# New-token attention: keys turned in blocks of 32 by VectorE, scores on 32 by 32 squares, values on quarters of the columns

## The chip, the cores and the metric

The kernel runs on one core of a Trainium2 chip. The core has five engines with instruction queues of their own: TensorE (PE in the profile, its weight loads PEld), VectorE (DVE), ScalarE (ACT), GpSimd (POOL) and SyncE (SP, which here only issues DMAs). TensorE multiplies on an array of 128 rows (the contracted index) by 128 columns (the output's partitions); a product can be put on a part of it. The metric is the device time of one launch in microseconds, median of three runs.

## The reference

A decoder step of two layers, on 512 prompt tokens and on eight sequences of eight new tokens each. The change is in the second layer's attention for the new tokens. Every new token has 16 heads of 64 in four groups (KV heads), and attends to three things: compressed keys, chosen blocks of 64 past keys, and a window of 512 keys. The last two are what the changed code computes:

```python
s = jnp.einsum('bqgrd,bqgksd->bqgrks', qg, kv_sel[..., 0, :])      # chosen blocks of the past 2048
p = masked_softmax(s, m.reshape(B, Q, KV_HEADS, 1, k_sel * SEL_BLOCK))
o_slc = jnp.einsum('bqgrks,bqgksd->bqgrd', p, kv_sel[..., 1, :])
s = jnp.einsum('bqgrd,bmgd->bqgrm', qg, wkv[:, :, 0])              # window
p = masked_softmax(s, wm[None, :, None, None, :])
o_win = jnp.einsum('bqgrm,bmgd->bqgrd', p.astype(wkv.dtype), wkv[:, :, 1])
o = g[..., 0:1] * o_cmp + g[..., 1:2] * o_slc + g[..., 2:3] * o_win
```

The kernel does not gather the chosen blocks: it computes the scores of all 2048 past keys and adds a large negative number to those of blocks not chosen. All of it is in 32-bit floats.

## The kernel before

The program runs these stages one after the other: pooling mixer, first feed-forward net, projections, compression of the past keys and values (`rounds`), new-token attention (`attend`), prompt attention, output projection, second feed-forward net. A scheduler orders the instructions of each engine, roughly as the code is written; a tile's buffer is handed on when its last reader has ended.

`attend` makes 40 steps, five for each of eight sequences b. Step 0 of a sequence is the window (512 rows of keys and values from `state_win_kv`), steps 1 to 4 are each 512 rows of the paged cache. A step's rows are one tile `sr` of 128 partitions, four rows in each, 1024 KB. `load` fetches it: the window by a DMA on SP, which also writes the shifted window to the output (`out_win_kv_s`, 1008 KB); the cache rows by a gather that POOL issues (L815). There are twelve such buffers, five in the pool `raws` that is open from earlier on, and seven (`more`) in memory that the stage before partly still uses.

- `prepare` (L1187 to L1201) turns the keys: eight PE transposes of 128 by 128 (`pk`), copied from PSUM to `kf` by ScalarE (two heads) and VectorE (the other two). It is done one step ahead.
- `score` (L1210 to L1235) multiplies them by the queries `qbd`, which hold two heads of 64 each on the rows and zeros in the other half: two products of 64 output partitions and 512 columns, side by side on the halves of the columns (`pss`). VectorE adds the mask and takes the maximum (`sc`, L1228, L1231). After step 0 and step 4 follows a softmax, whose exponential is one ScalarE instruction of 512 or 2048 elements (L1246).
- `turn` (L1252 to L1262) turns the probabilities back, four PE transposes (`ppt`), and `evac` copies them to `ph`, in turns by ScalarE and VectorE.
- `values` (L1265 to L1280): eight products of 64 by 128, on halves of the columns, into `po`. A pair of heads is multiplied with the values of both, so that half of each result is not used. They come six steps after the keys (four for the window), and are the last readers of `sr`.
- `outputs`, `outputs2`: the gates, and one transpose (`pot`) into `oS`.

All PSUM tiles of this and the stage before come from one group of eight banks (`any`). The weights of the output projection (`rawb`) and the prompt's keys and values (`kvt`) are loaded at the end of `attend`, as its memory comes free.

Of the kernel before, what the change touches and what calls it, by code (L numbers as in the profile page):

```python
# [60 lines left out]
def shape_constants():  # L61
# [36 lines left out]
    key = 4 * p[None, :] + np.arange(4)[:, None]  # L98
    parts["wm"] = np.where(key.reshape(1, -1) <= tt[:, None], NEG, 0.0)
# [30 lines left out]
def body(tc, top, I, O):  # L130
# [692 lines left out]
    def compress_setup(ctx):  # L823
# [21 lines left out]
        def buffers():  # L845
            xt = Z["xt"] = Slots(ctx, "xt", "right", hs=1, hgh=2, hgl=2, cvf=2)
            for n in range(XB):
                for tag in ("xf", "xhi", "xlo"):
                    xt.reserve(f"{tag}{n}", 1)
# [205 lines left out]
    def sample_attention(ctx):  # L1055
# [5 lines left out]
        VT = sa.tile([128, 2, 2, 128], F32, name="VT")  # L1061
# [12 lines left out]
        with ExitStack() as c1:  # L1074
# [6 lines left out]
            for j in range(2):  # L1081
                c0 = KC + 512 * (j + 1) + 256
                sp.dma_start(VT[64 * j:64 * j + 64, :, j], pjd[:, c0:c0 + 256].rearrange("t (a c) -> t a c", a=2))
# [102 lines left out]
        def prepare(i):  # L1186
# [5 lines left out]
            kf = kp_.tile([128, 2, 512], F32, tag="kf", name=f"kf{b}{ch}")  # L1192
            for p in range(2):
                pk = tpt(f"pk{b}{ch}{p}")
                for j in range(4):
                    transpose(pk[:, j * 128:(j + 1) * 128], raw[:, j, p * 128:(p + 1) * 128])
                if p:
                    dve.tensor_copy(kf[:, p], pk)
                else:
                    act.activation(kf[:, p], pk, AF.Copy)  # L1200
            kv[b, ch] = (kf, raw)  # L1201

        def attend(between):
# [4 lines left out]
            st, pend, po = {}, {}, {}  # L1208

            def score(i):  # L1210
# [13 lines left out]
                pt = mmt(f"pss{b}{ch}")  # L1224
                scores(pt, b, kf)
                if ch:
                    bias = sx[:, 128 * (ch - 1):128 * ch].unsqueeze(1).broadcast_to([128, 4, 128])
                    dve.tensor_tensor_reduce(sc[:, ch].rearrange("p (j k) -> p j k", j=4), pt.rearrange("p (j k) -> p j k", j=4),  # L1228
                                             bias, 1.0, -3e38, OP.add, OP.max, mx[:, ch - 1:ch])
                else:  # L1230
                    dve.tensor_tensor_reduce(sc[:, 0], pt, C("wm"), 1.0, -3e38, OP.add, OP.max, mx[:, 5:6])  # L1231
# [20 lines left out]
            def turn(b, ch):  # L1252
# [4 lines left out]
                for j in range(n):  # L1257
                    src = sc[:, ch, j * 128:(j + 1) * 128] if ch < 5 else (pcg[:, b] if j == 0 else pt_t)
                    transpose(pp[:, j * 128:(j + 1) * 128], src)
                ph = ptp.tile([128, 4, 128], F32, tag="ph", name=f"ph{b}{ch}")  # L1260
                evac(ph[:, :n].rearrange("p j c -> p (j c)"), pp[:, :n * 128])
# [3 lines left out]
            def values(b, ch):  # L1265
# [5 lines left out]
                for j in range(4 if ch < 5 else 2):  # L1271
                    for p in range(2):
# [515 lines left out]
```

## Time and profile before

| | us |
|---|---|
| median of 3 runs | 1693.01 (1692.02 to 1696.52) |
| profiled execution | 1694.61 |
| its span, first to last instruction | 1692.8 |
| PE busy in the span | 1628.4 (96%) |
| DVE, ACT, POOL busy | 1006.9, 766.5, 405.4 |
| mean granted clock of PE | 0.987 of 2.4 GHz |

The profile is of one execution. Its views: the page (busy times, groups of instructions by line), stretches (busy time of each engine in a window), the timeline, waits (who waited for whom) and DMA issues. A PE record is one pass: a 32-bit product shows as two records, a transpose as one. Records overlap, so how long a block takes is read from the start of the next one, not from its own duration. Times are counted from the span's start.

### The profile page before, as it was taken

How to read it: one execution, taken by the hardware profiler on the slowest of the kernel's cores; microseconds unless marked ns; L12 is line 12 of the kernel's file. 1: busy time of each engine (PE TensorE's matmuls, PEld its weight loads, DVE VectorE, ACT ScalarE, POOL GpSimd, SP SyncE). 2: the span in 40 equal slices, each digit the busy share in tenths (PEclk: the TensorE clock that was granted, in tenths of full speed). 3: DMA queues.
4: the chain of work that ended last, by engine and by line, in shares of the span. 5: the costliest groups of instructions: out<-in, count | busy, mean ns of one | idle time of the engine just before them, and what ended most of it. 6: DMA issues, size and time to landing. Idle time of an engine off the chain costs nothing. (4 is left out here: it accounts for less than half of the span.)

```text
span 1692.8 us, 31210 instructions
## 1 busy us (share of the span) xinstructions
PE 1628.4 (96%) x12663; PEld 1503.9 (89%) x12663; DVE 1006.9 (59%) x2052; ACT 766.5 (45%) x1400; POOL 405.4 (24%) x602
## 2 busy tenths in 40 slices
PE   8999999999999998999999998899999999999995
PEld 8999999999999998999966664556999999999995
DVE  7666364544474356888755547776456546454547
ACT  5655343343353324656554436666155524344331
POOL 3222021111020013334312206664023202111104
PEclk9999999999999998999999998999999999999998
DMA  5233133223246827454559971003312222222211
GB/s 191 84 101 100 51 100 101 75 76 100 64 138 213 253 88 282 156 190 168 181 179 348 341 204 25 1 2 90 94 51 97 79 75 94 82 82 78 91 60 57
DMA packets 121888, 204.95 MB, mean 121 GB/s; under 512 B 17327, under 2 KB 97289, under 8 KB 111376
## 3 DMA queue, kind: packets, MB, share of 16 engines
q1 hardware_dynamic: 111840, 133.45, 24.9%
q0 software_dynamic: 9216, 67.11, 11.0%
q10 hardware_dynamic: 688, 2.40, 0.4%
q8 instruction: 99, 1.62, 0.4%
q14 instruction: 45, 0.37, 0.1%
HBM read 178.58 MB, written 24.84 MB: 120 GB/s over the span
## 5 line engine op out<-in xcount | busy, mean ns | idle before, releaser
L166 PE MATMUL u<-xl,wha 128*128 128x288 f32 x704 | 208.1, 296 | 0.3 <-POOL xl L352 0.2
L166 PE MATMUL u<-xl,whb 128*128 128x288 f32 x704 | 208.1, 296 | 0.2
L166 PE MATMUL u<-xh,whb 128*128 128x288 f32 x704 | 207.4, 295 | 0.0
L166 PE MATMUL u<-xh,wha 128*128 128x288 f32 x704 | 207.4, 295 | 0.0
L166 PE MATMUL u<-xh,wla 128*128 128x288 f32 x704 | 207.3, 295 | 0.0
L166 PE MATMUL u<-xh,wlb 128*128 128x288 f32 x704 | 207.3, 295 | 0.0
L418 POOL COPY fcol<-u 128x18 f32<-128x18 f32 x88 | 68.4, 786 | 468.0 <-ACT u L417 468.0
L423 DVE SCALAR_TENSOR_TENSOR c<-u,convp,c 128x592 f32<-128x592 f32 x88 | 72.3, 831 | 122.5 <-ACT c L422 122.4
L258 DVE TENSOR_TENSOR wla<-rawa,wha 128x2048 fp32r<-128x2048 f32 (+1 forms) x52 | 99.5, 1918 | 69.3 <-ACT wha L257 69.3
L258 DVE TENSOR_TENSOR wlb<-rawb,whb 128x2048 fp32r<-128x2048 f32 x37 | 84.8, 2293 | 87.4 <-ACT whb L257 84.2
L166 PEld LDWEIGHTS u<-xl,wha 128*128 128x128 f32 x704 | 132.0, 188 | 2.0 <-DVE xl L352 1.1
L166 PEld LDWEIGHTS u<-xl,whb 128*128 128x128 f32 x704 | 132.0, 188 | 1.9 <-DVE xl L352 1.1
L166 PEld LDWEIGHTS u<-xh,wha 128*128 128x128 f32 x704 | 132.0, 188 | 0.1
L166 PEld LDWEIGHTS u<-xh,whb 128*128 128x128 f32 x704 | 132.0, 188 | 0.1
L166 PEld LDWEIGHTS u<-xh,wla 128*128 128x128 f32 x704 | 132.0, 188 | 0.0
L166 PEld LDWEIGHTS u<-xh,wlb 128*128 128x128 f32 x704 | 132.0, 188 | 0.0
L257 ACT ACTIVATE wha<-rawa 128x2048 fp32r<-128x2048 f32 (+1 forms) x52 | 83.0, 1615 | 91.3 <-PE d L166 58.9
L257 ACT ACTIVATE whb<-rawb 128x2048 fp32r<-128x2048 f32 x37 | 70.8, 1914 | 115.0 <-PE d L166 39.1
L504 DVE SCALAR_TENSOR_TENSOR xz<-xz,d 128x288 f32<-128x288 f32 x160 | 70.3, 450 | 86.7 <-PE d L166 85.9
L911 PE MATMUL pr<-xhi,W1h 128*128 128x256 f32 x512 | 105.6, 288 | 9.4 <-ACT xhi L884 9.4
L884 ACT ACTIVATE xhi<-xf 128x1024 fp32r<-128x1024 f32 (+1 forms) x68 | 70.1, 1031 | 80.0 <-PE pr L911 43.4
L882 DVE STREAM_TRANSPOSE xf<-cr 128x512 f32<-128x512 f32 x128 | 84.8, 691 | 33.9 <-POOL xlo L886 26.8
(657 smaller groups left out, 4640.6 us busy)
## 6 DMA issues: line engine op xcount, KB each, us to landing
rawa<-in_ffn_w_up SPq DMA_DIRECT2D x22, 1024.0 KB
rawb<-in_ffn_w_up SPq DMA_DIRECT2D x22, 1024.0 KB
rawa<-in_ffn_w_down SPq DMA_DIRECT2D x11, 1024.0 KB
rawb<-in_ffn_w_down SPq DMA_DIRECT2D x11, 1024.0 KB
rawa<-in_nsa_w_in SPq DMA_DIRECT2D x9, 1024.0 KB
sr<-in_state_win_kv SPq DMA_DIRECT2D x8, 1024.0 KB
out_win_kv_s<-sr SPq DMA_DIRECT2D x8, 1008.0 KB
rawb<-in_nsa_w_o SPq DMA_DIRECT2D x16, 256.0 KB
```

What stands on the lines that cost most here:

```text
L166: pe.matmul(out, a, b, start=first and j == 0, stop=last and j == n - 1)
L257: act.activation(h[:, a:b], r[:, a:b], AF.Copy)
L258: dve.tensor_tensor(lo[:, a:b], r[:, a:b], f32(h[:, a:b]), OP.subtract)
L418: pool.tensor_copy(col[:, :, m].rearrange("p (j i) -> p j i", i=2), u[:, TP:TP + 90].rearrange("p (j i) -> p j i", i=10)[:, :, 0:2])
L423: dve.scalar_tensor_tensor(c, u[:, 1:1 + CW], cv[:, 44 + m:45 + m], c, OP.mult, OP.add)
L504: dve.scalar_tensor_tensor(z, z, ALPHA if first else 1.0, p_[:, :HALF], OP.mult, OP.add)
L882: dve.transpose(xf[:, :, :, :, 32 * q:32 * q + 32].rearrange("p t d g n -> p t g d n"), src)
L884: act.activation(xhi.rearrange(flat), xf.rearrange(flat), AF.Copy)
L911: pe.matmul(banks[b, kv][ri][:, :, gh * nn:(gh + 1) * nn], W1[wi][:, kv, ri * 8 + th * 4 + c], xx[:, c // 2, c % 2].rearrange("p g n -> p ...
```

## The change

The keys no longer go through PE. One VectorE instruction turns each 32 by 32 block of a step's keys where it stands, so that the 64 elements of a head come to lie as two halves f of 32 rows, in each of the four row groups q of the array, and a row group holds 128 of the step's 512 keys. The queries are brought into the same form once (`qq`): sixteen small DMAs put them into rows of four heads by eight tokens, three DMAs repeat them for the other row groups, and VectorE turns them. The scores are then 32 products of 32 rows, 32 columns (a KV head's four heads by eight tokens) and 128 keys: for both halves f, each row group q and each KV head g one, on the square (q, g) of the array. Each row group writes into a bank of its own, and a step takes a quarter of each of four banks, in turn (`ring`). Keys are now numbered by partition first, so the mask of the window, the mask's broadcast and the slices of `turn` change to match.

The values become 16 products of 64 columns, one per KV head on its quarter of the columns, without the unused half. `ph` is copied by ScalarE alone. `outputs` works on 64 columns, and writes the result twice for the transpose. PSUM is opened anew for `attend`: four banks for the ring, four for all else. One tile of the compression stage (`xlo2`) is reserved first, which moves the others in memory.

```diff
--- before.py
+++ after.py
@@ -95,8 +95,7 @@
     parts["cm1"] = cm.reshape(128, -1)
     parts["cma"] = ((cm - 1.0) * np.float32(-NEG)).reshape(128, -1)
     tt = p % 8
-    key = 4 * p[None, :] + np.arange(4)[:, None]
-    parts["wm"] = np.where(key.reshape(1, -1) <= tt[:, None], NEG, 0.0)
+    parts["wm"] = np.where(np.arange(512)[None, :] <= tt[:, None], NEG, 0.0)
     tm = np.where(np.arange(8)[None, :] <= tt[:, None], 0.0, NEG)
     parts["tm"] = np.concatenate([tm, tm], 1)
     gt = (p // 32) * 8 + tt
@@ -844,9 +843,10 @@
 
         def buffers():
             xt = Z["xt"] = Slots(ctx, "xt", "right", hs=1, hgh=2, hgl=2, cvf=2)
-            for n in range(XB):
-                for tag in ("xf", "xhi", "xlo"):
-                    xt.reserve(f"{tag}{n}", 1)
+            last = f"xlo{XB - 1}"
+            for tag in [last] + [f"{tag}{n}" for n in range(XB) for tag in ("xf", "xhi", "xlo")]:
+                if tag not in xt.bufs:
+                    xt.reserve(tag, 1)
 
         def rows_of(b):
             raw = []
@@ -1058,7 +1058,9 @@
 
         qf = sa.tile([128, NB, 2, 64], F32, name="qbd")
 
-        VT = sa.tile([128, 2, 2, 128], F32, name="VT")
+        VT = sa.tile([128, 4, 2, 64], F32, name="VT")
+
+        qq = sa.tile([128, NB, 4, 2, 32], F32, name="qq")
         stl = sa.tile([128, NB, 16], F32, name="stl")
         selb = sa.tile([128, NB, 34], F32, name="selb")
         pcg = sa.tile([128, NB, 128], F32, name="pcg")
@@ -1080,7 +1082,16 @@
                 sp.dma_start(kjs[:, j], pjd[:, KC + 512 * (j + 1):KC + 512 * (j + 1) + 256])
             for j in range(2):
                 c0 = KC + 512 * (j + 1) + 256
-                sp.dma_start(VT[64 * j:64 * j + 64, :, j], pjd[:, c0:c0 + 256].rearrange("t (a c) -> t a c", a=2))
+                sp.dma_start(VT[64 * j:64 * j + 64, :, j], pjd[:, c0:c0 + 256].rearrange("t (g c) -> t g c", g=4))
+
+            q4 = s1.tile([128, NB, 4, 64], F32, name="q4")
+            for r in range(4):
+                for g in range(4):
+                    c0 = g * 256 + r * 64
+                    sp.dma_start(q4[8 * r:8 * r + 8, :, g], pjd[:, c0:c0 + 64].rearrange("(b t) c -> t b c", t=TS))
+            for q in range(1, 4):
+                sp.dma_start(q4[32 * q:32 * q + 32], q4[0:32])
+            dve.transpose(qq.rearrange("p b g f n -> p (b g f) n"), q4.rearrange("p b g (f i) -> p (b g f) i", f=2))
             qr = s1.tile([64, 2, 4, 2, 64], F32, name="qr")
             for p in range(2):
                 dve.tensor_copy(qr[:, p].rearrange("t r e c -> t e r c"),
@@ -1189,15 +1200,9 @@
             b, ch = steps[i]
             prepared.add(i)
             raw = raws.pop(i)
-            kf = kp_.tile([128, 2, 512], F32, tag="kf", name=f"kf{b}{ch}")
-            for p in range(2):
-                pk = tpt(f"pk{b}{ch}{p}")
-                for j in range(4):
-                    transpose(pk[:, j * 128:(j + 1) * 128], raw[:, j, p * 128:(p + 1) * 128])
-                if p:
-                    dve.tensor_copy(kf[:, p], pk)
-                else:
-                    act.activation(kf[:, p], pk, AF.Copy)
+
+            kf = kp_.tile([128, 2, 4, 128], F32, tag="kf", name=f"kf{b}{ch}")
+            dve.transpose(kf.rearrange("p f g (n j) -> p j g f n", j=4), raw[:, :, 0:256].rearrange("p j (g f i) -> p j g f i", g=4, f=2))
             kv[b, ch] = (kf, raw)
 
         def attend(between):
@@ -1206,6 +1211,8 @@
             scp = Slots(ctx, "ss", sc=2, ptail=2, mx=3, sx=2, cvb=2, osb=2)
             ptp = Slots(ctx, "sp", ph=3)
             st, pend, po = {}, {}, {}
+
+            ring = mmt("pss", "s", 4)
 
             def score(i):
                 b, ch = steps[i]
@@ -1221,14 +1228,21 @@
                     sp.dma_start(cvb, cvd[b])
                     st[b] = (sc, pt_t, mx, sx, cvb)
                 sc, pt_t, mx, sx, _ = st[b]
-                pt = mmt(f"pss{b}{ch}")
-                scores(pt, b, kf)
+                pt = ring[:, :, (i % 4) * 128:(i % 4 + 1) * 128]
+                for f in range(2):
+                    for q in range(4):
+                        for g in range(4):
+                            qs = slice(32 * q, 32 * q + 32)
+                            pe.matmul(pt[32 * g:32 * g + 32, q], qq[qs, b, g, f], kf[qs, f, g], start=f == 0, stop=f == 1,
+                                      tile_position=(32 * q, 32 * g))
+                by_key = "p (q n j) -> p q n j"
                 if ch:
-                    bias = sx[:, 128 * (ch - 1):128 * ch].unsqueeze(1).broadcast_to([128, 4, 128])
-                    dve.tensor_tensor_reduce(sc[:, ch].rearrange("p (j k) -> p j k", j=4), pt.rearrange("p (j k) -> p j k", j=4),
-                                             bias, 1.0, -3e38, OP.add, OP.max, mx[:, ch - 1:ch])
+                    bias = sx[:, 128 * (ch - 1):128 * ch].rearrange("p (q n) -> p q n", q=4).unsqueeze(3).broadcast_to([128, 4, 32, 4])
                 else:
-                    dve.tensor_tensor_reduce(sc[:, 0], pt, C("wm"), 1.0, -3e38, OP.add, OP.max, mx[:, 5:6])
+                    bias = C("wm").rearrange(by_key, j=4, q=4)
+                m = ch - 1 if ch else 5
+                dve.tensor_tensor_reduce(sc[:, ch].rearrange(by_key, j=4, q=4), pt.rearrange("p q (n j) -> p q n j", j=4),
+                                         bias, 1.0, -3e38, OP.add, OP.max, mx[:, m:m + 1])
                 if ch == 0:
                     softmax(b, 1, 5, 7, 0, 1)
                 if i % 5 == 4:
@@ -1255,10 +1269,10 @@
                 n = 4 if ch < 5 else 2
                 pp = tpt(f"ppt{b}{ch}")
                 for j in range(n):
-                    src = sc[:, ch, j * 128:(j + 1) * 128] if ch < 5 else (pcg[:, b] if j == 0 else pt_t)
+                    src = sc[:, ch].rearrange("p (k j) -> p j k", j=4)[:, j] if ch < 5 else (pcg[:, b] if j == 0 else pt_t)
                     transpose(pp[:, j * 128:(j + 1) * 128], src)
                 ph = ptp.tile([128, 4, 128], F32, tag="ph", name=f"ph{b}{ch}")
-                evac(ph[:, :n].rearrange("p j c -> p (j c)"), pp[:, :n * 128])
+                act.activation(ph[:, :n].rearrange("p j c -> p (j c)"), pp[:, :n * 128], AF.Copy)
                 pend[b, ch] = ph
 
 
@@ -1269,23 +1283,28 @@
                     po[b] = mmt(f"po{b}")
                 raw = kv.pop((b, ch))[1] if ch < 5 else None
                 for j in range(4 if ch < 5 else 2):
-                    for p in range(2):
+                    for g in range(4):
                         if ch < 5:
-                            v, c0 = raw[:, j, 256 + 128 * p:384 + 128 * p], 128 if ch == 0 else 0
+                            v, c0 = raw[:, j, 256 + 64 * g:320 + 64 * g], 64 if ch == 0 else 0
                         elif j == 0:
-                            v, c0 = cvb[:, 128 * p:128 * p + 128], 256
+                            v, c0 = cvb[:, 64 * g:64 * g + 64], 128
                         else:
-                            v, c0 = VT[:, p].rearrange("q s c -> q (s c)"), 0
-                        pe.matmul(po[b][64 * p:64 * p + 64, c0:c0 + v.shape[1]], ph[:, j, 64 * p:64 * p + 64], v,
-                                  start=ch == 0 and j == 0, stop=ch == 5 and j == 1)
+                            v, c0 = VT[:, g].rearrange("q s c -> q (s c)"), 0
+                        rs = slice(32 * g, 32 * g + 32)
+                        pe.matmul(po[b][rs, c0:c0 + v.shape[1]], ph[:, j, rs], v,
+                                  start=ch == 0 and j == 0, stop=ch == 5 and j == 1, tile_position=(0, 32 * g))
 
             def outputs(b):
-                osb = scp.tile([128, 128], F32, tag="osb", name=f"osb{b}")
+                osb = scp.tile([128, 3, 64], F32, tag="osb", name=f"osb{b}")
                 mx = st[b][2]
-                act.activation(osb, po[b][:, 256:384], AF.Copy)
-                for j in (1, 0):
-                    dve.scalar_tensor_tensor(osb, po[b][:, 128 * j:128 * j + 128], mx[:, 11 + 4 * j:12 + 4 * j], osb, OP.mult, OP.add)
-                return osb
+                tmp = osb[:, 2]
+                act.activation(tmp, po[b][:, 128:192], AF.Copy)
+                dve.scalar_tensor_tensor(tmp, po[b][:, 64:128], mx[:, 15:16], tmp, OP.mult, OP.add)
+
+                twice = [128, 2, 64]
+                dve.scalar_tensor_tensor(osb[:, 0:2], po[b][:, 0:64].unsqueeze(1).broadcast_to(twice), mx[:, 11:12],
+                                         tmp.unsqueeze(1).broadcast_to(twice), OP.mult, OP.add)
+                return osb[:, 0:2].rearrange("p s c -> p (s c)")
 
             def outputs2(b, osb):
                 pt = tpt(f"pot{b}")
@@ -1735,9 +1754,11 @@
                 elif i == 6:
                     fn["select2"](1, sel[1])
 
+            cb.close()
+            cb = c1.enter_context(ExitStack())
+            open_banks(cb, 3, s=1, any=4)
             fn["attend"](between)
         cs.close()
-        cb.close()
         c0 = top.enter_context(ExitStack())
         open_x(c0, 1)
         U = Units(c0, "b")
```

In the order of PE, names are tile, then sequence and step: pk310 and pk311 are the turned keys of sequence 3, step 1, pss31 its scores, ppt22 the turned probabilities of sequence 2, step 2, po2 the values' sum of sequence 2. Before, from the scores of sequence 3, step 1:

```order
L1109 MATMUL pss31_10910<-kf31_10847,qbd_7617 64x512 x2
L203 MATMUL ppt21_10914<-cst_58,sc2_10649 128x128 x4
L203 MATMUL pot1_10921<-cst_58,osb1_10891 128x128
L203 MATMUL pk330_10928<-cst_58,sr33_10748 128x128 x4
L203 MATMUL pk331_10934<-cst_58,sr33_10748 128x128 x4
L1109 MATMUL pss32_10940<-kf32_10897,qbd_7617 64x512 x2
L203 MATMUL ppt22_10944<-cst_58,sc2_10649 128x128 x4
L1279 MATMUL po2_10835<-sr21_10477,ph21_10919 64x128 x8
L203 MATMUL pk340_10962<-cst_58,sr34_10789 128x128 x4
L203 MATMUL pk341_10968<-cst_58,sr34_10789 128x128 x4
L1109 MATMUL pss33_10974<-kf33_10927,qbd_7617 64x512 x2
L203 MATMUL ppt30_10978<-cst_58,sc3_10860 128x128 x4
```

After, from the same scores:

```order
L1236 MATMUL pss_10295<-kf31_11220,qq_7619 32x128 x32
L202 MATMUL ppt21_11335<-cst_58,sc2_10877 128x128 x4
L202 MATMUL pot1_11342<-cst_58,osb1_11294 128x128
L202 MATMUL ppt22_11383<-cst_58,sc2_10877 128x128 x3
L1236 MATMUL pss_10295<-kf32_11300,qq_7619 32x128 x32
L202 MATMUL ppt22_11383<-cst_58,sc2_10877 128x128
L1294 MATMUL po2_11200<-sr21_10612,ph21_11340 32x64 x16
L202 MATMUL ppt30_11443<-cst_58,sc3_11222 128x128
L1236 MATMUL pss_10295<-kf33_11348,qq_7619 32x128 x32
L202 MATMUL ppt30_11443<-cst_58,sc3_11222 128x128 x3
L202 MATMUL ppt23_11450<-cst_58,sc2_10877 128x128 x4
L1294 MATMUL po2_11200<-sr22_10656,ph22_11388 32x64 x16
```

The `pk` rows are gone, a score is 32 products and a value 16, and the scores now stand between transposes that stood together: from `pss31` to `pss40` the array's division changes fourteen times in a sequence, where it changed sixteen times.

In the order of VectorE, the end of sequence 2 (ISA is the masked sum with its maximum, then the reading of the maximum). Before:

```order
L1228 ISA sc2_10649,mx2_10651<-pss24_10804,sx2_10653 128x512
L1228 ISA mx2_10651 128x1
L212 COPY ph14_10820<-ppt14_10815 128x512
L1243 TENSOR_REDUCE mx2_10651<-mx2_10651 128x1
L1198 COPY kf31_10847<-pk311_10854 128x512
L1248 TENSOR_TENSOR mx2_10651<-mx2_10651 128x1
L1249 RECIPROCAL mx2_10651<-mx2_10651 128x1
L1231 ISA sc3_10860,mx3_10862<-pss30_10868,cst_58 128x512
L1231 ISA mx3_10862 128x1
L1250 TENSOR_TENSOR mx2_10651<-mx2_10651,gsm_5908 128x1
L1243 TENSOR_REDUCE mx3_10862<-mx3_10862 128x1
```

After:

```order
L1244 ISA mx2_10879 128x1
L1205 STREAM_TRANSPOSE kf30_11130<-sr30_10872 128x4x4x2x32
L1244 ISA sc2_10877,mx2_10879<-pss_10295,sx2_10881 128x512
L1244 ISA mx2_10879 128x1
L1205 STREAM_TRANSPOSE kf31_11220<-sr31_10953 128x4x4x2x32
L1257 TENSOR_REDUCE mx2_10879<-mx2_10879 128x1
L1262 TENSOR_TENSOR mx2_10879<-mx2_10879 128x1
L1244 ISA sc3_11222,mx3_11224<-pss_10295,cst_58 128x512
L1244 ISA mx3_11224 128x1
L1263 RECIPROCAL mx2_10879<-mx2_10879 128x1
L1205 STREAM_TRANSPOSE kf32_11300<-sr32_11001 128x4x4x2x32
L1264 TENSOR_TENSOR mx2_10879<-mx2_10879,gsm_5908 128x1
```

The transposes stand where the copies of `kf` stood, a step ahead of the scores that they feed, and the copy of `ph` is gone; a masked sum now stands behind the transpose of the step after it.

In the order of POOL, the gathers of the first sequences (`cr` is the compression's, `sr` the attention's). Before, at the beginning of the compression:

```order
L815 DMA sr14_10395<-in_cache_slc_kv,idx_6274 128x2048
L1065 MEMSET qbd_7617 128x1024
L1066 MEMSET VT_7618 128x512
L1067 MEMSET pcg_7621 128x8
L1071 MEMSET ohb_7629 128x512
L1118 MEMSET pce0_8034 128x4
L1150 MEMSET sel0_9054 128x34
L815 DMA sr13_10369<-in_cache_slc_kv,idx_6274 128x2048
L1073 COPY ohb_7629<-cst_58 128x32 x4
L815 DMA sr11_10310<-in_cache_slc_kv,idx_6274 128x2048
L815 DMA sr12_10329<-in_cache_slc_kv,idx_6274 128x2048
```

After, at its end:

```order
L814 DMA sr04_9930<-in_cache_slc_kv,idx_6274 128x2048
L886 TENSOR_TENSOR xlo8101_10121<-xf8101_10119,xhi8101_10120 128x512
L814 DMA sr14_10486<-in_cache_slc_kv,idx_6274 128x2048
L1224 MEMSET ptl0_10300 128x128
L1226 COPY sx1_10556<-selb_7621 128x512
L1226 COPY sx0_10303<-selb_7621 128x512
L1224 MEMSET ptl1_10553 128x128
L814 DMA sr21_10612<-in_cache_slc_kv,idx_6274 128x2048
L1158 MEMSET m11_10433 128x3
L814 DMA sr22_10656<-in_cache_slc_kv,idx_6274 128x2048
```

Before, all four gathers of sequence 1 were issued early (sr14 first); now sr14 stands at the end of the compression, behind sr04.

## Rows read from the trace of the kernel before

**Rows 1.** Stretches: us; busy us (instructions) of PE, PEld, DVE, ACT, POOL; clock; DMA share; GB/s.
```profile
860.00:870.00 10.00, 8.97 (x60) 5.57 (x60) 7.26 (x28) 6.19 (x12) 0.43 (x2) 1.00 0.16 64
...
880.00:890.00 10.00, 10.00 (x100) 7.14 (x98) 4.07 (x9) 4.06 (x7) 3.39 (x5) 1.00 0.67 224
890.00:980.00 90.00, 90.00 (x817) 60.10 (x817) 51.78 (x154) 38.57 (x88) 21.16 (x28) 1.00 0.93 345
980.00:990.00 10.00, 10.00 (x98) 6.74 (x97) 6.35 (x21) 5.99 (x15) 0.20 (x1) 1.00 0.29 114
```

**Rows 2.** Stretches, one sequence of five steps.
```profile
908.60:927.20 18.60, 18.60 (x173) 12.55 (x175) 10.49 (x31) 8.18 (x20) 4.54 (x7) 1.00 0.94 344
```

**Rows 3.** Timeline of PE and PEld: start, us, line, what, count, idle before.
```profile
916.23 1.09 PE L1279 MATMUL po<-sr,ph 128*64 128x128 f32 x16
...
917.25 1.09 PE L203 MATMUL pk<-cst,sr 128*128 128x128 f32 x8
...
918.27 1.08 PE L1109 MATMUL pss<-kf,qbd 128*64 128x512 f32 x4
...
919.28 1.09 PE L203 MATMUL ppt<-cst,sc 128*128 128x128 f32 x8
...
920.30 1.09 PE L1279 MATMUL po<-sr,ph 128*64 128x128 f32 x16
...
923.75 0.14 PEld L203 LDWEIGHTS ppt<-cst,pcg 128*128 128x128 f32 x1
...
923.86 0.14 PEld L203 LDWEIGHTS ppt<-cst,ptl 128*128 128x128 f32 x1
```

**Rows 4.** Waits in the stage: who waited for whom, us, times, longest.
```profile
POOL sr L815 <- PE po L1279: 71.8, 22, 7.1
```

**Rows 5.** Timeline of POOL: gathers of the keys and values.
```profile
880.42 0.94 POOL L815 DMA_INDIRECT sr<-in_cache_slc_kv,idx  x1 [7.12 <-PE po L1279]
...
977.46 0.94 POOL L815 DMA_INDIRECT sr<-in_cache_slc_kv,idx  x1 [3.14 <-PE po L1279]
```

**Rows 6.** DMA issues of the stage: count, median us to landing.
```profile
sr<-in_cache_slc_kv,idx POOLq DMA_INDIRECT x24, 8.2
```

**Rows 7.** Groups by shape in the stage: busy us, mean ns; idle before.
```profile
L1198 DVE COPY kf<-pk 128x512 f32<-128x512 f32 x40 | 27.6, 690 | 40.9 <-PE pk L203 29.9 <-issue 10.7
...
L212 DVE COPY ph<-ppt 128x512 f32<-128x512 f32 x23 | 15.8, 688 | 0.5 <-PE ppt L203 0.4
...
L1200 ACT ACTIVATE kf<-pk 128x512 f32<-128x512 f32 x40 | 23.6, 592 | 21.7 <-PE pk L203 19.3 <-issue 2.3
L1246 ACT ACTIVATE sc<-sc,mx 128x2048 f32<-128x2048 f32 x8 | 16.0, 2004 | 18.0 <-DVE mx L1243 18.0
```

**Rows 8.** The page, part 5: the block transposes of the stage before.
```profile
L882 DVE STREAM_TRANSPOSE xf<-cr 128x512 f32<-128x512 f32 x128 | 84.8, 691 | 33.9 <-POOL xlo L886 26.8
```

**Rows 9.** Timeline of PE in prompt attention: halves, then quarters of the columns.
```profile
1116.27 1.03 PE L1519 MATMUL pop<-pc,cvp 128*64 128x512 f32 x4
1117.23 1.07 PE L1411 MATMUL pk<-Q,KB 128*32 128x512 f32 x8
1118.23 0.66 PE L203 MATMUL ppp81a<-cst,P 128*128 128x128 f32 x4
```

**Rows 10.** Stretches in prompt attention around a fall of the clock.
```profile
1132.00:1138.30 6.30, 3.82 (x27) 1.86 (x26) 3.96 (x18) 3.13 (x13) 3.19 (x4) 1.00 0.00 0
1138.30:1141.70 3.40, 3.34 (x14) 2.10 (x14) 2.55 (x5) 1.49 (x6) 2.38 (x4) 0.50 0.00 0
```

**Rows 11.** Instructions of the scores: ns min/median/max, first and last start.
```profile
L1109 PE MATMUL pss<-kf,qbd x160: 592/593/644, 859.0 to 996.1; 128*64 128x512 f32 x160
```

**Rows 12.** Timeline of the end of the stage.
```profile
995.62 1.03 PE L1109 MATMUL pss<-kf,qbd 128*64 128x512 f32 x4
...
1000.27 2.03 SPq L1339 DMA_DIRECT2D kvt<-kvd  x4
...
1010.56 0.65 PE L203 MATMUL pkp<-cst,kvt 128*128 128x128 f32 x4
```

## The prediction

> **What bounds the kernel now.** I went from the whole to the stage. The page says PE is busy nearly throughout, so what counts is what PE does in the stage that the change touches: eight sequences of five steps each, on the trace from 859.0 us (first score product [rows 11]) to 1010.56, where PE takes up the next stage [rows 12]. The view by stretches over one sequence (18.6 us) has PE busy for all 18.6, VectorE for 10.49 and ScalarE for 8.18, with the DMA engines at a share of 0.94 and 344 GB/s [rows 2]. The reader is to see two things there: PE is the engine that never waits, and the DMA engines are almost full beside it. The timeline then says what PE does: one step is four blocks of about 1.02 us, namely the values (16 records), the turning of the keys (8 transposes), the scores (4 records of 512 columns) and the turning of the probabilities [rows 3]. Last the waits: the gathers, issued on POOL, were held by PE's value products for 71.8 us in 22 waits [rows 4]. So PE paces, the buffers carry its pace to the DMA engines, and before the steady part they idle: share 0.16 in 860 to 870 and 0.67 in 880 to 890 against 0.93 after that [rows 1].
>
> **The change part by part.** All sums are per sequence (five steps), then over the stage.
>
> *Keys turned by VectorE.* PE loses five key blocks of 1.02 us [rows 3]: 5.1 us. VectorE loses five copies of 0.690 and three of 0.688 [rows 7], 5.5 us, and gains five block transposes of 1024 elements per row. The nearest row is the same instruction on 512 elements, 0.691 us [rows 8]; twice that is 1.38, which I take; the fixed part counted twice makes it a little too high. The new ones write every fourth element, which no row shows: bounds 1.2 and, if that halves the rate, 2.76. VectorE then has 10.49 - 5.5 + 6.9 = 11.9 us (17.6 at most with 2.76: 18.8). That is 2.4 us a step, beside PE.
>
> *Scores on squares.* 32 products of 128 columns, two records each as now, so 64 records. A record of 128 columns on the whole array is followed by the next after 0.11 us (923.75 to 923.86 [rows 3]). Quarters of the columns do run side by side: eight records of 512 columns on quarters fill 1.00 us, as four on halves fill 0.96 [rows 9]. Nothing shows sixteen squares at once. Bounds for the block: 64 / 16 x 0.11 = 0.43 if all sixteen run together, 64 / 4 x 0.11 = 1.76 if only the four quarters do, 64 x 0.11 = 7.0 if none. I take 0.85, with pairs of row groups together, and keep the others for the range.
>
> *Values on quarters.* 32 records of 64 columns, so 0.055 each, four together by [rows 9]: 0.44 a step, against some 0.87 of the 1.02 now.
>
> *Order changes on PE.* Eight transposes take 8 x 0.11 = 0.88 of a block of 1.02 [rows 3]: about 0.15 goes at each change of the array's division. By the order below there are fourteen such changes in a sequence where sixteen were: 2.1 us. With 23 transposes (2.5), five scores (4.25), five values (2.2) and the last two small products (0.3), PE has 2.1 + 2.5 + 4.25 + 2.2 + 0.3 = 11.3 us in a sequence instead of 18.6. With scores at 1.76 it is 15.9.
>
> The Trainium skill (TensorE: Matmul & The Clock Gate, Back-to-back issue gap) speaks against so many small products: starts never come closer than about 25 ns, however few the columns. By that a score block would be 1.6 and a value block 0.8, an estimate, and PE 16.9 us in a sequence. The same page (Measured speedup vs the span model) has sixteen squares ending some 4 ns apart, and by that a score block is nearer 0.7. No run here decides between them; by either the sum below stays as it is.
>
> *ScalarE* loses five passes of 0.592 and gains three probability copies of at most 0.69: below 8.18 us. But one pass of 2.0 us [rows 7] now stands ahead of every copy, and PE has two or three free banks for turned probabilities where it had more. Cost nothing, hidden by PE's spare 6 us; if the cover were gone, 2.0 us a sequence.
>
> *Where the time then goes.* Neither PE (11.3) nor VectorE (11.9) paces the full part any more; the DMA engines do. From 880 to 990 they moved 10 x 0.224 + 90 x 0.345 + 10 x 0.114 = 34.4 MB [rows 1]. At 344 GB/s for a share of 0.94 [rows 2], a full share is 366; I take 362, so 95.0 us. This stream starts when the value products of the eighth step free a buffer: now at 880.42 [rows 5], 21.4 us after 859.0. At VectorE's 2.4 us a step, 7.3 steps make 17.5: start at 876.5. End of the last gather: 971.5, where now it is 977.46 [rows 5] + 8.2 to landing [rows 6] = 985.7. That is 14.2 us earlier.
>
> *The tail.* Now the last score starts at 995.62 [rows 12], 9.9 us after the last data landed, since PE lags. Then it follows the landing by one transpose and a score's wait, 1.6 us: 8.3 us more. From that score to the first product of the next stage are 14.9 us (995.62 to 1010.56 [rows 12]). In it the next stage's loads are issued (1000.27) and land; I leave it at 14.9, though PE's share of it shrinks (4 us less) and the weights that now load before it, in a gap of the DMA engines, may queue in it (6 us more).
>
> *Small parts.* One gather of the second sequence is no longer issued early but at the stage's start: 1 MB in a stretch where the DMA engines have a share of 0.16 [rows 1], so nothing; uncovered, 2.9 us. Nineteen small DMAs on SP and a VectorE transpose of 2048 elements (2.8 us) for the queries stand 200 us ahead of use. Behind them on SP wait only result rows and the first window loads, with all that time in hand: nothing, 3 us if PE's products there had to wait. The scores' four banks are taken all at once at the start: nothing, up to 3 us; the sixteen key transposes ahead of 859.0 that go (1.8 us) stand against that.
>
> **The sum.** 14.2 + 8.3 = 22.5 us off the profiled span of 1692.8, which with the 1.8 around it makes the execution of 1694.6: 1672.1. The profiled run is 1.6 above the median of 1693.0, so 1670.5, rounded to 1671.
>
> **Rivals.**
> 1. *PE's clock falls.* For the first time PE idles in every step. After 6.3 us in which PE was busy for 3.82, the granted clock fell to 0.50, that is 1.2 GHz, from 1138.3 to 1141.7; there PE was busy for 3.34 of 3.40, and then the clock was back [rows 10]. At half the clock a sequence needs 22.6 us, above the 17.7 that the DMA engines need (five loads of 1024 KB, a write of 1008 KB and 128 KB of values, 6.4 MB, at 362); but only if the clock is low for over 72% of the time is PE the slower one (11.3 / (1 - 0.72 / 2) = 17.7). What is left is the ramp and the tail, which have no slack: 5 to 9 us. Time 1679.
> 2. *The transfers give less back.* The first steps wait for their chain of engines, so that the stream starts no earlier than 880.42, and the DMA engines stay at 345 GB/s: 99.7 us, end at 980.1, 5.6 earlier instead of 14.2; the weights queue in the tail, 6 more. For it: 344 GB/s is all that a sequence reached. Against: the share was 0.94, held by buffers, not by the engines. Time 1694.6 - 5.6 - 8.3 + 6 - 1.6 = 1685.
> 3. *Slower: the squares don't overlap.* The place is the score block, in all forty steps. If records on parts of the array follow each other no faster than those on halves now (16 in 0.87 us, 0.054 each [rows 3]), a score is 3.5 us, a value block 1.7, and PE has 11.3 + 5 x (2.65 + 1.3) = 31 us a sequence, 12.4 more than now: 8 x 12.4 = 99 us, time 1792. It decides from 36 ns a record on (PE above 18.6). Against it: the quarters of [rows 9] overlap. For it: no row has more than four pieces of the array at work.
> 4. *The change does not do what it says*: the keys leave PE and VectorE takes as long for them. With writes at half the rate it needs 18.8 us a sequence where PE needed 18.6, and the stage keeps its length: 1693, 1 or 2 more or less. Against: the transposes of today write runs of 32 elements at 0.691 us for 512 [rows 8], as a plain copy does (0.690 [rows 7]), so the turning itself costs nothing extra.
>
> **How the numbers follow.** Forecast 0.56 (own range 1661 to 1678: tail -4 to +6, rate 355 to 375, start of the stage 3 either way), rival 1 0.10, rival 2 0.16, rival 3 0.13, rival 4 0.05. The measurement tells about 0.3%, 5 us, from no change. Faster by more: the forecast, rival 1 and most of rival 2, 0.80. Within: rival 4 and the end of rival 2, 0.06. Slower: rival 3 and a little of the rest, 0.14. The range from 1661 to 1691 leaves out rival 3 and a few in a hundred on either side.
>
> **What would show it.** Right: in a middle sequence PE busy clearly below the stretch, the DMA share at 0.97 or more, a sequence of 17 to 18 us, transposes of the keys near 1.3 us each, score blocks below 1.8 us, VectorE's key transposes now waiting for a DMA, the last gather issued near 963. Wrong: PE still busy throughout with score blocks above 2 us (rival 3); transposes near 2.7 us and PE waiting for VectorE (rival 4); a granted clock of 0.5 over much of the stage (rival 1); an attention stage that ends early while the next one still starts at its old distance from the last landing. The forecast falls altogether if a sequence still takes 18.6 us.

## The result: slower by 1.6%, and the profile after

The changed kernel takes 1719.72 us (median of 4 runs, 1718.97 to 1727.31) against 1693.54 for the kernel before: ratio 1.0162, 95% interval 1.0130 to 1.0195. The forecast was 1671. The profiled execution took 1727.3 us and has a span of 1725.5, 32.7 longer than before; it was the slowest of the four, so that its trace shows some 6 us more loss than the medians (26.2).

The first view is the one by stretches, with the columns of [rows 1]: first the stretches of that group, then 890 to 976, then the rest of the stage, which now lasts beyond its old end.

```profile
860.00:870.00 10.00, 7.42 (x252) 5.32 (x267) 9.49 (x23) 0.60 (x1) 1.10 (x3) 0.62 0.16 30
880.00:890.00 10.00, 7.33 (x254) 4.95 (x236) 6.35 (x9) 4.33 (x8) 2.68 (x4) 0.98 0.87 306
890.00:980.00 90.00, 65.24 (x1858) 45.21 (x1846) 55.24 (x107) 24.14 (x58) 15.55 (x20) 0.69 0.74 259
980.00:990.00 10.00, 8.43 (x314) 5.72 (x313) 5.36 (x10) 4.28 (x9) 3.62 (x5) 0.91 0.80 274
890.00:976.00 86.00, 61.24 (x1784) 42.43 (x1773) 54.03 (x104) 23.84 (x57) 14.62 (x19) 0.70 0.75 266
990.00:1011.00 21.00, 16.40 (x545) 11.68 (x520) 15.66 (x30) 7.48 (x18) 2.08 (x3) 0.79 0.70 257
1011.00:1035.00 24.00, 20.47 (x602) 15.21 (x584) 10.79 (x28) 9.84 (x23) 0.46 (x2) 0.76 0.77 191
```

In the middle stretch nothing is full: PE is busy for 65 of 90 us, VectorE for 55, the DMA engines at a share of 0.74 where they had 0.93. The number in brackets is what grew: 1858 records on PE and 1846 on its weight loads, 817 of each before. The last gather is issued at 1002.25 (977.46 before, [rows 5]) and prompt attention begins at 1036.55 (1010.56, [rows 12]): 26 of the 32.7 us lie in the stage, the other 6.7 after it, where the granted clock was low for 34 us instead of 17 (the last 20 us of the program left out); the code there is the same.

Who keeps PE waiting? The waits of PE and PEld from 890 to 976, and the timeline of PE over two steps:

```profile
PE pss L1236 <- issue: 23.8, 13, 3.5
PEld pss L1236 <- issue: 29.3, 26, 3.7
PEld po L1294 <- ACT ph L1275: 1.4, 4, 0.4
```

```profile
915.11 1.86 PE L1236 MATMUL pss<-kf,qq 32*32 32x128 f32 x56
919.54 0.42 PE L1236 MATMUL pss<-kf,qq 32*32 32x128 f32 x8 [2.57 <-issue]
...
921.55 1.52 PE L1236 MATMUL pss<-kf,qq 32*32 32x128 f32 x64
...
923.42 0.80 PE L1294 MATMUL po<-sr,ph 128*32 128x64 f32 x32
...
924.46 0.43 PE L1236 MATMUL pss<-kf,qq 32*32 32x128 f32 x13
926.25 0.95 PE L1236 MATMUL pss<-kf,qq 32*32 32x128 f32 x51 [1.35 <-issue]
```

No engine releases PE: the wait is "issue". And it stands in the middle of a score block, after 56 records once and after 13 the next time, where the program has no wait at all. Counting what TensorE did between two such stops (127 or 128 matmul records on PE, as many weight loads on PEld, and one or two instructions of its sequencer) gives 256 each time, for 14 stops in a row from 894 to 976. The DMA queue that the page calls "instruction" explains the number: q8, one packet of 16,384 bytes at a time, that is 64 bytes for each of 256 instructions. The page counts 121 packets (99 before); from 890 to 976 there are 14:

```profile
q8 instruction: 14, 0.23, 0.9%
```

Set side by side, packet by packet, in us:

```
last record   packet starts   lands     next record   landing to next
   910.72        910.77       911.71       913.06          1.35
   916.55        917.28       918.22       919.54          1.32
   924.63        923.92       924.84       926.25          1.41
   930.67        929.81       930.78       932.02          1.24
   934.61        935.58       936.54       937.92          1.38
```

PE resumes 1.2 to 1.6 us after the packet has landed, in all stops. The packet itself takes 0.95 us, and starts 2.8 to 4.6 us after the previous stop ended; in the two places below, where the DMA engines had less to do (shares of 0.07 and 0.50 between the stop's end and the packet), after 1.1 and 1.5.

```profile
976.00:977.10 1.10, 1.10 (x40) 0.71 (x41) 0.00 (x0) 0.00 (x0) 0.41 (x1) 0.50 0.07 15
1026.70:1028.20 1.50, 1.50 (x52) 1.29 (x55) 0.48 (x3) 0.43 (x2) 0.46 (x2) 1.00 0.50 191
```

All this fits one picture: PE has no more than one block of 256 instructions ahead, asks for the next at about the time that it begins a block, and under this load can go on with it 5.1 to 7.0 us later, 6.16 on average. It uses up a block in some 4 us. That is theory A: instructions are supplied at 256 per 6.16 us, and a sequence that needs 1038 of them (matmul records and weight loads together) takes 25 us, whatever the engines could do. The trace has 24.6 where 18.6 stood [rows 2]. Before, a sequence had 348 and so needed a packet every 14 us; no idle time of PE in that trace ends as these stops do.

The Trainium skill (Runtime: NRT & Kernel Launch, Instruction fetch mechanics) says the blocks are of 256 instructions and that crossing one is mostly hidden. The trace agrees on the block; here the crossing is not hidden.

Two other readings had to be told apart from A. Theory B: the clock. It is 0.70 in the stretch (1.2 GHz for some 60% of it) and was 1.00 before; a score block without a stop takes 1.07 us at full clock and 1.99 at half, from its first start to its last end, by two rows of PE's timeline:

```profile
989.66 1.07 PE L1236 MATMUL pss<-kf,qq 32*32 32x128 f32 x64
997.24 1.99 PE L1236 MATMUL pss<-kf,qq 32*32 32x128 f32 x64
```

Theory C: VectorE. A key transpose takes 2.04 us instead of the forecast's 1.38:

```profile
L1205 DVE STREAM_TRANSPOSE kf<-sr 128x1024 f32<-128x1024 f32 x19 | 38.7, 2036 | 0.0
```

### The profile page after: what moved, and what is told of

Read it like the earlier page. It is cut to its first block, busy times and chain, and to the rows that moved or that the text cites. A ratio compares the mean times of both kernels' runs of the same rounds, so it can differ in the third digit from the quotient of the medians.

```text
span 1725.5 us, 36745 instructions
## 1 busy us (share of the span) xinstructions
PE 1625.2 (94%) x15447; PEld 1504.4 (87%) x15447; DVE 1044.1 (61%) x2029; ACT 758.7 (44%) x1384; POOL 405.0 (23%) x602
## 3 DMA queue, kind: packets, MB, share of 16 engines
q1 hardware_dynamic: 113392, 134.49, 24.7%
## 4 chain that ended last, share of the span: by engine, by line
PE 79%; issue 7%; DVE 7%; POOL 4%; ACT 3%; DMA 1%; SPq 0%; ACTq 0%; POOLq 0%; DVEq 0%
PE u L165 31%; PE d L165 14%; PE pr L911 10%; PE pj L165 7%; PE pss L1236 3%; PE wo L165 2%; POOL P L1505 2%; PE ppt L202 2%; PE psp L1486 1%; PE po L1294 1%; PE pop L1534 1%; PE pj L709 1%; DVE kf L1205 1%; DVE wla L257 1%; DVE lnst L320 1%
## 5 line engine op out<-in xcount | busy, mean ns | idle before, releaser
L911 PE MATMUL pr<-xlo,W1h 128*128 128x256 f32 x512 | 104.6, 286 | 2.7 <-DVE xlo L886 2.7
L165 PE MATMUL d<-hh,wha 128*128 128x288 f32 x352 | 104.4, 298 | 0.1
```

The costliest lines, as they stand in the source:

```text
L165: pe.matmul(out, a, b, start=first and j == 0, stop=last and j == n - 1)
L911: pe.matmul(banks[b, kv][ri][:, :, gh * nn:(gh + 1) * nn], W1[wi][:, kv, ri * 8 + th * 4 + c], xx[:, c // 2, c % 2].rearrange("p g n -> p ...
```

## The experiments

Ratios are against the kernel before, run on the same chip (1694.2 to 1694.4 us), with 95% intervals.

**Values alone.** The kernel before with the `values`, `outputs` and `VT` of the changed one; keys and scores untouched.

> The kernel before with the values on quarters alone; keys and scores as they were. Theory A (TensorE's instructions arrive in blocks of 256, one fetch ahead, some 6 us from one to the next while the DMA engines are loaded): a sequence has about 510 instructions on TensorE, two blocks or 12 us, so no stall; TensorE's 18.6 us a sequence fall to some 16.2 and the DMA engines (17.7) pace: 1671 to 1685 us. Theory B (small squares and idle time drop the clock, and the array at 1.2 GHz is what paces): TensorE now idles, the clock falls, 1693 us or more.

1681.04 us, 0.9918 (0.9902 to 0.9935).

```profile
890.00:976.00 86.00, 85.72 (x1335) 53.78 (x1324) 53.69 (x168) 42.30 (x99) 21.15 (x28) 1.00 0.95 371
```

Half of the change is good by itself. PE stays at full clock and the DMA engines carry 371 GB/s where they carried 345 [rows 1]. Of the kernels that compute the reference this is the fastest, and beats both.

**Old products on the turned keys.**

```
-  32 products, 32x32, 128 columns each
+  scores(bank, b, kf.rearrange("p f g c -> p f (g c)"))
```

> The changed kernel, but its score products are the two of the kernel before (512 columns on halves), on the keys as VectorE turned them, so the scores have no meaning; everything else stays. Theory A: about 440 instructions a sequence instead of 1038, 1.7 blocks, 10 us: no stall; the DMA engines pace, 1670 to 1685 us. Theory B: TensorE idles in each step, the clock stays at 0.5, and a sequence takes about 20 us: 1700 to 1710. Theory C (VectorE's key transposes of 2.04 us, in a chain with the scores and two key buffers, pace): no better than the changed kernel, 1710 to 1720.

1684.18 us, 0.9938 (0.9921 to 0.9954).

```profile
890.00:976.00 86.00, 71.26 (x1145) 35.85 (x1143) 73.67 (x142) 36.23 (x83) 22.73 (x30) 1.00 0.98 383
```

and what PE waits for in it:

```profile
PE pss L1120 <- DVE mx L1240: 6.8, 12, 1.2
```

The key transposes are all there (2.08 us each) and VectorE is busy for 74 of 86 us, yet the "issue" waits are gone from PE's list, the DMA engines are at a share of 0.98 and the kernel is 35.5 us faster than the changed one. C falls. B's rule, that idle time alone keeps the clock low, falls as well: PE idles for 15 us here at 1.00.

**The same instructions, a sixteenth of the columns.**

```
- pe.matmul(pt[32 * g:32 * g + 32, q], qq[qs, b, g, f], kf[qs, f, g], ...
+ pe.matmul(pt[32 * g:32 * g + 32, q, 0:8], qq[qs, b, g, f], kf[qs, f, g, 0:8], ...
```

> The changed kernel with its 32 score products on 8 of their 128 columns (the rest of the scores is a constant from one fill at the start): the same instructions, a sixteenth of their columns. Theory A: as many blocks of 256 as before, the stalls grow by what the products lose, 1712 to 1722 us. Theory B: the score block falls from 1.1 to 2.2 us to a third of that, some 0.8 us a step at least: 1690 us or less. Theory C: 1715 to 1720.

1715.74 us, 1.0130 (1.0113 to 1.0147).

```profile
890.00:976.00 86.00, 57.61 (x1906) 44.92 (x1907) 53.22 (x104) 26.11 (x60) 16.51 (x23) 0.60 0.81 291
```

```profile
PE pss L1237 <- issue: 19.5, 8, 4.7
```

Fifteen sixteenths of the columns of the scores are gone, and 4 us of 26. The stops are fewer and longer, up to 4.7 us: all "issue" waits of PE together are 25.5 us where the changed kernel has 26.8. The columns in the array are not what paces. The weight loads are as many as before, so this run does not speak of them.

**The same columns, half the instructions.**

```
-  for f in range(2): ... 32 products of 128 columns, kf[qs, f, g]
+  16 products of 256 columns, kf[qs, :, g]
```

> The changed kernel with 16 score products of 256 columns on the same sixteen squares instead of 32 of 128 (the second half of the features isn't added, so the scores have no meaning): the same columns in the array, half the score instructions. Theory A: 718 instructions a sequence, 2.8 blocks, 17 us: 1675 to 1692 us. Theory B: the array does the same at the same clock: 1712 to 1722. Theory C: 1715 to 1720.

1683.33 us, 0.9939 (0.9922 to 0.9955).

```profile
890.00:976.00 86.00, 67.25 (x1830) 40.84 (x1799) 73.89 (x147) 35.87 (x84) 20.39 (x27) 0.82 0.95 362
```

```profile
PE pss L1236 <- issue: 2.2, 2, 1.1
```

The mirror of the run before: the columns stay, and 36 us go; PE's "issue" waits are 5.2 us in all. The weight loads of the scores are halved with them; in the changed kernel all weight loads together kept PEld busy for 42 of 86 us. The clock is still low for a third of the stretch, and that costs nothing that can be seen, since the DMA engines pace again.

**Values back on halves**, the scores on squares as changed:

> The changed kernel with the value products back on halves (16 records a step instead of 32): 862 instructions a sequence on TensorE instead of 1038. Theory A (blocks of 256 instructions, 6.05 us each): 20.4 us a sequence instead of 24.5, five sequences of the stage are so paced: 1695 to 1705 us, although the array works longer. Theory B (array time at the low clock): a value block takes 0.4 to 0.8 us more: 1735 to 1750.

1701.57 us, 1.0050 (1.0025 to 1.0075): 18 faster than the changed kernel although the array does more for each value block. The sequences take 18.2 to 20.8 us.

```profile
890.00:976.00 86.00, 69.92 (x1951) 52.68 (x1948) 70.70 (x133) 30.75 (x73) 19.11 (x25) 0.96 0.93 343
```

```profile
PE pss L1236 <- issue: 3.2, 3, 2.2
```

The time is in A's range, but this run does not part A from the clock: the stops have shrunk to 4.1 us in all, and the clock is 0.96 instead of 0.70.

**DMA engines nearly idle.**

> The changed kernel, in which from the thirteenth load on every load brings 32 of 128 rows (256 KB; the other rows stay from an earlier load) and windows are neither loaded nor written back from there: the same instructions on TensorE, DMA engines nearly idle. Theory A: the fetch of 256 instructions comes sooner, some 3.5 us (1.1 to 1.5 to its start as in the two cases beside idle DMA engines, 0.95, 1.4) instead of 6.05, 14 us a sequence, so that the array and VectorE pace (16 to 19 us): 1670 to 1690. Theory B: the clock stays at 0.5, a sequence takes 22 us, 1705 to 1715. Theory C: 1715 to 1720.

1695.54 us, 1.0005 (0.9991 to 1.0020): 24 faster than the changed kernel, 5 above A's range.

```profile
890.00:976.00 86.00, 72.68 (x2430) 52.27 (x2439) 70.50 (x135) 32.19 (x75) 22.26 (x31) 0.78 0.29 78
```

```profile
q8 instruction: 19, 0.31, 1.5%
```

```profile
PE pss L1239 <- issue: 1.6, 4, 0.6
```

With the same instructions and a DMA share of 0.29 the stops in score blocks shrink from 23.8 to 1.6 us, and a sequence takes 18.1. A packet comes every 4.5 us instead of 6.16, which is now the pace at which PE uses the blocks up. The fetch itself is quicker than that: counting on by 256 from stop to stop, a packet starts 0.0 to 2.7 us after a block begins (median 1.0, 19 blocks) where it started after 2.8 to 4.6 (median 3.9). So it is the kernel's own transfers that make the fetch late. What fills the 18.1 us then isn't one engine: PE is busy for 85% of the time at a clock of 0.78, VectorE for 82%. That the low clock is what A left out here is likely, but not shown.

**Dummies in the good kernel.** Values alone, with 27 more products of 8 columns a step ahead of the scores:

> The kernel with values on quarters alone (1681 us) and 27 more products in each step, of 8 columns on squares of 32, whose sums are overwritten: 108 more instructions on TensorE a step, 1050 a sequence as in the changed kernel, hardly more columns. Theory A: the stalls come back, 24 us a sequence, 1715 to 1735 us. Theory B or plain issue cost (64 records at 7 to 17 ns, 0.4 to 0.9 us a step on TensorE, which had 1.3 us a sequence to spare): 1690 to 1705.

1721.36 us, 1.0148 (1.0128 to 1.0169): in A's range, and yet no proof.

```profile
890.00:960.00 70.00, 64.76 (x1672) 43.99 (x1661) 33.53 (x97) 24.88 (x56) 14.57 (x19) 0.95 0.79 283
```

Its trace has PE busy for 65 of 70 us and only a few of the stops; the dummies cost PE 0.6 us a step, and its first steps ran at the low clock (0.52 from 860 to 870). Packets come every 5.4 us from 890 to 976, and the sequences take 20.5 to 25.2 us. Inconclusive; it does show that 6 us a block is not a fixed rate.

**The write step of the key transposes**, in the changed kernel and with the old products:

```
- kf.rearrange("p f g (n j) -> p j g f n", j=4)
+ kf.rearrange("p f g (j n) -> p j g f n", j=4)
```

> The changed kernel, whose key transposes write runs of 32 elements instead of every fourth one (the keys' columns then stand in another order than the masks and values, so the output has no meaning). The transpose's own time tells where 2.04 us for 1024 elements come from: 1.38 if it is the write step, as twice the 0.691 of the 512-element transposes; 2.04 if it is the count or the reading. Theory A (instruction supply paces): the total stays, 1712 to 1722 us, since VectorE's 0.65 us a step were beside the stalls. Theory C (VectorE's transposes pace): 1690 to 1700.

> The kernel with the old score products on the turned keys (1684 us, no instruction stalls, VectorE busy for 60 of 70 us), its key transposes writing runs of 32 elements. If the write step costs 0.65 us a transpose, the first eight steps, which VectorE fills, take 5 us less, the gathers start so much earlier, and the total falls to 1677 to 1681; if the transposes stay at 2.04, 1682 to 1686.

1715.37 us, 1.0130 (1.0111 to 1.0150), as A said, and 1673.80 us, 0.9878 (0.9862 to 0.9895), 3 below the range. The transposes of the second:

```profile
L1205 DVE STREAM_TRANSPOSE kf<-sr 128x1024 f32<-128x1024 f32 x26 | 32.3, 1242 | 6.2 <-DMA sr<-in_cache_slc_kv,idx 4.3 <-PE ppt L202 1.8
```

Writing every fourth element costs 0.8 us in each transpose. With the squares that is worth 4 us, hardly more than the noise, without them 10.4: it counts where instructions don't pace. And the two kernels differ in nothing but the score products: 41.6 us.

**The whole change mended**: scores for two steps at once, and contiguous writes, with ScalarE's exponential putting the keys back in order, into a tile of its own; the mask is read without the widened copy `sx`. Values on quarters, then on halves.

> The whole change again, with two things mended. Scores are computed for two steps at once (32 products of 256 columns for a pair, of 128 for the fifth step), so a sequence has 96 score products instead of 160 and some 782 instructions on TensorE instead of 1038; and the key transposes write runs of 16 elements, with ScalarE's exponential putting the keys back in order. Theory A (blocks of 256 at 6.05 us): 18.5 us a sequence, still a little over what the DMA engines need (16.5 to 17.7): 1680 to 1695. Theory B (array at the low clock): no better than 1705.

> The same with the values on halves as in the kernel before: 606 instructions a sequence, 2.4 blocks, 14.3 us, below the DMA engines' 16.5 to 17.7. Theory A: no stalls, 1673 to 1684, faster than the one with values on quarters although the array does more. Theory B: slower than that one, over 1705.

1695.94 us, 1.0011 (1.0001 to 1.0021), and 1698.77 us, 1.0023 (1.0007 to 1.0040). Better than the changed kernel by 24 and 21, but both miss A's range, by 1 and by 15. In the first the sequences take 17.8 to 19.0 us, as A said. In the second the stops for instructions are gone; from 890 to 976 another wait took their place:

```profile
PE po L1304 <- ACT ph L1286: 12.8, 8, 2.7
```

```profile
L1271 ACT ACTIVATE ex<-sc,mx 128x2048 f32<-128x2048 f32 x5 | 20.0, 4003 | 3.5 <-DVE mx L1267 3.5
```

The exponential, now writing every fourth element, takes 4.00 us instead of 2.00 [rows 7], and the probability copies queue behind it, once a sequence. But most of the two misses lies elsewhere. The last gathers are issued at 971.3 and 972.6, beside 970.5 with the old products. From there to prompt attention it takes 35.4 and 39.3 us (31.0 there), and from there to the end 687.7 and 686.3 (681.0 there), where the clock was low for 27 and 24 us (14 there; the last 20 us left out again). How much of the tail is the slower exponential was not tested.

## Why the prediction was wrong

The step that failed is the one before the sum: *neither PE nor VectorE paces the full part any more; the DMA engines do*. The 64 records of a score block were counted as time in the array, and two rules on how closely they may start were weighed with the remark that *by either the sum below stays as it is*. That they must also be brought to PE was in no term and in no rival, though the page of before has the queue, 99 packets of 16 KB. What the runs showed in its place: beside the stage's transfers PE got 256 instructions in 6.16 us, so that the 1038 of a sequence took some 25 us where the forecast had 17.7 for the DMA engines; these stood at a share of 0.74, and their gathers waited for PE. The sum for it could have been made in part: 1038 records a sequence against 348 [rows 2]. How late a packet comes could not be read from a wait in the trace of before, since there none was ever waited for.

Three runs part the loss: the old products on contiguously turned keys take 1673.8, close to the forecast; writing every fourth element adds 10.4 (1684.2); the score products in 32 small squares add 35.5 (1719.7). That the first is so close is in part luck: its last gather was issued 8 us before the forecast's 963, and from it to prompt attention (988.1) it took 32.5 us where the forecast had 24.7.

- *Keys leave PE*: right; no turning of keys is left on it.
- *Key transposes 1.38 us*: 2.04, inside its bounds; of its reasons the one named as not shown by any row, the write of every fourth element, is the cause (1.24 without it). VectorE was busy for 9.49 of 10 us in the first steps (860 to 870), and the gather that came at 880.42 came at 878.4, 2 us earlier and not 3.9. Even that is owed to an earlier start: the first score came at 854.3 instead of 859.0, and from it to the gather it is 24.1 us, not 17.5.
- *Squares overlap*: right, against rival 3. Sixty-four records took 1.00 us to the next block's start (row at 989.66; 1.07 to their last end), 16 ns each, above the 0.85 taken; at 1.2 GHz 1.5 to 2.0. That is some seven records at a time on average (none overlapping would be 7.0 us); it does not show all sixteen squares at once. The 25 ns between starts that the Trainium skill gives (TensorE: Matmul & The Clock Gate, Back-to-back issue gap) do not hold for these squares.
- *Values on quarters*: 0.58 us a block at full clock (1031.40 to 1031.98), 0.44 taken; as an edit by itself it gives 13 us.
- *Transfers 95.0 us from their start*: the engines can do it: 383 GB/s with the old products, where 362 was taken. In the run with old products and contiguous writes the last gather was issued at 955.6, before the 963 that was asked for. In the changed kernel they were held by PE, as before: the gathers waited 57.1 us for value products from 890 to 976.
- *The tail*: 14.9 us from the last score was taken; it is 14.7 (1021.80 to 1036.55). The 8.3 us ahead of it did not come: from the issue of the last gather to the last score it is 19.6 us (1002.25 to 1021.80), not 9.8, since PE lagged as before.
- *Rival 1, the clock*: it fell as the rival feared, but stops that end when a packet lands are not the clock's doing. After 976, where the stops are rare, steps take 4.1 us (3.72 before) at a clock of 0.76 to 0.91, so some of the loss is its own; how much was not separated.
- *Rivals 2 and 4* fell: the DMA engines give more than 345 GB/s (383), and VectorE with its 2.04 us was busy for 55 of 90 us.
- *Rival 3* had the sign and nearly the culprit, many small products; its mechanism and its 1792 were wrong. The chance of 0.14 for slower had no room for a bound that isn't an engine.
- Two slips in the sums decide nothing: the 17.6 beside VectorE's 18.8 comes from no row, and the 36 ns from which rival 3 decides counts the score records alone (with the value records, which its sum has too, 28.5).

Of the signs named in advance, the DMA share (0.74, not 0.97), the sequence (24.6, not 17 to 18) and the last gather (1002, not 963) all say that the forecast fell, and none of the causes listed there, PE busy throughout, transposes at 2.7, a low clock alone, is the one.

## What to carry to other kernels

Count instructions as a resource of their own: divide those that an engine issues in a stage by 256, multiply by the time that a fetch takes beside the stage's transfers (6.2 us here; with the transfers cut some 3.5, an estimate from a median of 2.1 from a block's begin to the landing and 1.4 more to PE), and compare with the time of the stage. For TensorE count the weight loads too. The result is a rough bound: for the run with dummies it gives 25 us, which took 20.5 to 25.2. Small tiles that overlap well in the array can lose to a few large ones for that reason alone. In a profile, an idle time "issue" in the middle of a block without waits, at a fixed count of records, is its mark.

## What the runs showed of the hardware

- TensorE stopped after every 256 instructions (14 times in a row) where it used them up faster than a 16 KB packet came; it resumed 1.2 to 1.6 us after the landing.
- The packet comes later beside the kernel's transfers: it starts 2.8 to 4.6 us after a block begins at a DMA share of 0.75, 0.0 to 2.7 at 0.29. Why it is delayed by so much was not tested.
- A block transpose of 1024 elements takes 1.24 us with runs of 16 or 32 elements written, 2.04 with every fourth; the exponential of 2048 elements 2.00 and 4.00.
- More than four squares of 32 by 32 run side by side: 64 records of 128 columns in 1.00 us, some seven at a time; a record on the whole array is followed by the next after 0.11 us [rows 3].
